# A two-layer diffusion backbone on one core: the first expert layer adds its gated results straight to the stored tokens

## The chip, the core and the metric

The kernel runs on one core of one Trainium2 chip. The metric is the device time of one execution in microseconds (us), the median of the runs; lower is better. Five engines work side by side: PE (TensorE, matmuls), DVE (VectorE), ACT (ScalarE), POOL (GpSimd) and SP (SyncE, which here only issues DMAs). SBUF is the memory on the core, PSUM holds what matmuls write, DRAM is the chip's large memory.

## The reference

768 tokens of 1024 numbers (256 context tokens, then 512 latent ones) pass through two layers. Each layer has a mixer (attention) and a mixture of 32 experts, of which every token uses two. Cut to what matters here:

```python
for l in range(2):
    x = x + gt1 * o_lat                       # mixer; ctx likewise with cgt1 where not last
    if l == 0:
        tokens = concat([modulate(ctx, ...csh2, csc2), modulate(x, ...sh2, sc2)])
        f = hier_moe(tokens, ...)             # 768 tokens
        ctx = ctx + cgt2 * f[:256]            # the context's gate row
        x = x + gt2 * f[256:]                 # the latent tokens' gate row
    else:
        f = hier_moe(modulate(x, ...), ...)   # 512 tokens
        x = x + gt2 * f
# hier_moe: y = (silu(x @ w1[e]) * (x @ w3[e])) @ w2[e];  f = sum over the token's two experts of weight * y
```

The two gate rows cgt2 and gt2 hold 1024 numbers each, one per column. A token's gate depends only on whether it is a context or a latent token, so gating each expert's result before the sum gives the same f as gating the sum.

## The kernel before

Tokens lie in SBUF as `oo`, six tiles of 128 tokens (tiles 0 and 1 are context). Stages, by the time of the profile: first mixer (0 to 400 us), its output projection with the router (to 494), MoE of layer 0 (to about 1042), a hand-over, second mixer `mixer_c` (differential attention, to about 1470), its output projection with the router (to 1543), MoE of layer 1 (to the end).

**MoE.** Each expert has 6 MB of weights (w1, w3, w2), which stream from DRAM through slots of 1 MB (`wr`, `oo` reused). An expert with up to 64 tokens is "small": its tokens are gathered as half rows (128 x 512, tiles `xg`); eight others, the two "static" ones first and six "big" ones, are gathered as 96 rows of 1024 (`xgb`). Per expert: POOL gathers the rows by an indirect DMA (`gather`, L1518); PE transposes them (`trx`), DVE or ACT copies them out (`x`); PE multiplies with w1 and w3 (`h`); ACT takes silu (`sl`), DVE the product (`gp`); PE transposes (`trg`), then multiplies with w2 (`py`, two PSUM buffers); `weigh` multiplies with the tokens' router weight, from PSUM to `y` in SBUF; POOL scatters `y` by an indirect DMA that adds (`scatter`, L1525). Scatters of one layer wait for one another's landing, since they add to the same DRAM tensor. In layer 0 `weigh` is one ACT instruction per 512 columns (L1532) and the scatter adds to `yd`, a DRAM tensor of sums that was set to zero early in the kernel (`no_sums`, L836). In layer 1 `weigh` is one DVE instruction that also multiplies with the gate row (L1534), and the scatter adds straight to the output, which holds the tokens by then.

**Hand-over.** `xd` (`source(1, t)`) is DRAM with the tokens as they were before MoE 0. Near the end of MoE 0 the ACT queue loads them back to `oo` (six DMAs of 512 KB, L1722) and SP loads the two gate rows (`next_rows`, L505) and the first weights of `mixer_c` (`next_weights`, L1743). A branch follows that joins all engines (`overflow`, L1757; its body, for experts that overflow their table, does not run here). Then `mixer_c` (L1851 to L1910) loads the sums from `yd`, multiplies them by the gates (DVE for tile 0, POOL for tiles 1 to 5, L1886), adds them to `oo` (DVE, L1889), stores the four latent tiles back to `xd` (L1904), squares and sums each tile (ACT, L1892), finds the reciprocal root (`rstd`, nine small DVE instructions, L285 to L297), scales (ACT, L1910), and `flip_mod` transposes the tile on PE (`ht`, L646), modulates it (`h`, L655/L657) and splits it in two parts of matmul operands (`chh`, `chl`). With the first column blocks of the weights split in the same way (`wh`, `wl`, L323) PE starts the projections (`pp`, L262 to L264).

**Order.** Within each stage a list scheduler in the kernel's own code (`Sched`) writes the instruction order of PE, DVE, ACT and POOL: every step has an engine, an assumed time, the steps that it depends on, a due position (`S.pos`), and buffers that it takes and gives. SP's DMAs keep the order of the code. Each engine runs its list strictly in order.

Of the kernel before, what the change touches and what calls it, by code (L numbers as in the profile page):

```python
# [12 lines left out]
I32 = mybir.dt.int32  # L13
# [35 lines left out]
GATES = 1  # L49
# [187 lines left out]
class Backbone:  # L237
# [94 lines left out]
    def setup(self):  # L332
# [26 lines left out]
        self.yd = [tc.dram_tile([NTOK, D], F32, name="yd")]  # L359
# [409 lines left out]
    def mixer_ab(self):  # L769
# [52 lines left out]
        def second_stage():  # L822
# [7 lines left out]
            c.zero = one.tile([128, 64], F32, name="zero")  # L830
            nc.sync.dma_start(c.sink, i["sink_a"][0].partition_broadcast(128))
            nc.gpsimd.tensor_scalar(c.nsink, c.sink, -1.0, None, op0=OP.mult)
            nc.gpsimd.memset(c.zero, 0.0)
# [37 lines left out]
        for t in range(NT):  # L871
            S.op("DMA", 0.1, lambda t=t: no_sums(t), [closed], pos=n - APREP + t)
# [148 lines left out]
    def prepare_out(self, l, wout, pos, after):  # L1021
# [6 lines left out]
        def room():  # L1028
# [3 lines left out]
                "idx": t("idx", [128, NST], I32), "sw": t("sw", [128, NST]), "ps": t("ps", [CAP, 2, NE]),  # L1032
                "ord": t("ord", [1, NE], I32), "idx2": t("idx2", [128, NE], I32), "sw2": t("sw2", [128, NE]),
                "idxb": t("idxb", [CAP, 8], I32), "swb": t("swb", [CAP, 8]), "base": t("base", [128, NE]), "nb": t("nb", [NE, 2]), "ad": t("ad", [128, 2 * NT], I32),
# [30 lines left out]
    def out_proj(self, l, oo, first, gain=None):  # L1065
# [10 lines left out]
        with ExitStack() as st:  # L1076
# [158 lines left out]
            def index():  # L1235
# [4 lines left out]
                V.tensor_copy(r["sw"][:CAP], pslot[:, 1, 0:NST])  # L1240
                nc.scalar.copy(r["ps"], pslot)

# [66 lines left out]
    def route(self, l, j, nt, x, v, deps, sb, psp, pslot, summed, placed):  # L1309
# [5 lines left out]
        def t(name, *sh):  # L1315
            if name not in T:
                T[name] = sb.tile([128, *sh], F32, tag="r_" + name, name=name)
            return T[name]
# [59 lines left out]


    def sort_experts(self, l, nt):  # L1380
        nc, V, cst, r = self.nc, self.nc.vector, self.cst, self.rt
        with tc_pools(self.tc, ("sos", 1, {}), ("sop", 1, {"space": PSUM})) as (sb, ps):
# [28 lines left out]
            nc.scalar.copy(r["sw2"], p2[:, 1])  # L1411
# [3 lines left out]
            nc.scalar.copy(r["swb"], p3[:, 1])  # L1415
# [74 lines left out]
    def moe(self, l, nt, oo):  # L1490
# [3 lines left out]
        with ExitStack() as st:  # L1494
# [7 lines left out]
            gate = None  # L1502
            if l == 1:
                gate = one.tile([128, DE], F32, name="g2"), one.tile([CAP, D], F32, name="g2b")
                for h in range(2):
                    nc.sync.dma_start(gate[0][CS * h:CS * h + CS],
                                      self.modrow[1][0, 5 * D + DE * h:5 * D + DE * h + DE].partition_broadcast(CS))
                nc.sync.dma_start(gate[1], self.modrow[1][0, 5 * D:6 * D].partition_broadcast(CAP))
            xgs = [one.tile([128, DE], F32, name=f"xg{j}") for j in range(NX)]
            xgb = [one.tile([CAP, D], F32, name=f"xgb{j}") for j in range(2)]  # L1510
# [602 lines left out]
```

## Time and profile before

| what | value |
|---|---|
| median of 3 runs | 2069.01 us (2067.35 to 2069.65) |
| profiled execution | 2068.61 us |
| its span in the trace | 2066.8 us |
| busy: PE / DVE / ACT / POOL | 1795.9 / 935.4 / 561.1 / 336.2 us |
| DMA moved | 541 MB, mean 262 GB/s |

The span is what the trace covers from the first to the last record; 1.8 us of the profiled execution lie outside it. All times in the rows are of the profiled execution, counted from the span's start. A row of the timeline gives start, duration, engine, line, operation, output<-inputs, the count of like instructions, and in brackets the idle time before it and what ended it. "ACTq" or "SPq" mark the queue part of an engine, which issues DMAs; there the duration is the time of issuing, not of the transfer. A row of a window gives its length, then the busy time of each engine in it (with counts), the clock that TensorE was granted (1.00 is its upper level), the busy share of the DMA engines and what they moved. MoE stages are bounded by the weight stream, mixers by PE; how far that holds for the stretches that the change touches is in the rows below.

### The profile page before, as it was taken

How to read it: one execution, taken by the hardware profiler on the slowest of the kernel's cores; microseconds unless marked ns; L12 is line 12 of the kernel's file. 1: busy time of each engine (PE TensorE's matmuls, PEld its weight loads, DVE VectorE, ACT ScalarE, POOL GpSimd, SP SyncE). 2: the span in 40 equal slices, each digit the busy share in tenths (PEclk: the TensorE clock that was granted, in tenths of full speed). 3: DMA queues.
4: the chain of work that ended last, by engine and by line, in shares of the span. 5: the costliest groups of instructions: out<-in, count | busy, mean ns of one | idle time of the engine just before them, and what ended most of it. 6: DMA issues, size and time to landing. Idle time of an engine off the chain costs nothing. (4 is left out here: it accounts for less than half of the span.)

```text
span 2066.8 us, 26429 instructions
## 1 busy us (share of the span) xinstructions
PE 1795.9 (87%) x9506; PEld 1060.8 (51%) x9506; DVE 935.4 (45%) x2496; ACT 561.1 (27%) x1281; POOL 336.2 (16%) x358
## 2 busy tenths in 40 slices
PE   4999998896999988989838999996878998898896
PEld 2798776684333332323327988886763332232232
DVE  4698878585111111111168878776781211111111
ACT  4564566321001000001045555554310000000000
POOL 2000000002112111111042322224121211111111
PEclk8999999897999999999969999998988999999999
DMA  8702314437899999999952223231449999999996
GB/s 331 261 25 91 123 45 163 154 133 260 333 381 394 407 402 404 396 408 406 369 194 75 72 85 129 74 116 36 179 182 356 357 397 413 411 412 414 413 412 262
DMA packets 111016, 541.23 MB, mean 262 GB/s; under 512 B 34451, under 2 KB 34819, under 8 KB 55585
## 3 DMA queue, kind: packets, MB, share of 16 engines
q1 hardware_dynamic: 95584, 515.30, 63.7%
q0 software_dynamic: 14432, 21.05, 4.3%
q10 hardware_dynamic: 864, 3.15, 0.4%
q8 instruction: 77, 1.26, 0.2%
q14 instruction: 59, 0.48, 0.1%
HBM read 521.12 MB, written 34.28 MB: 269 GB/s over the span
## 5 line engine op out<-in xcount | busy, mean ns | idle before, releaser
L1628 PE MATMUL h<-wr,x 128*64 128x512 f32 x1584 | 405.1, 606 | 70.1 <-DMA wr<-in_w_dram 69.8
L1628 PEld LDWEIGHTS h<-wr,x 128*64 128x64 f32 x1584 | 117.0, 137 | 284.6 <-issue 158.6
L1603 DVE COPY x<-trx 128x512 f32<-128x512 f32 (+1 forms) x74 | 47.4, 649 | 457.2 <-PE trx L1598 452.4
L1652 ACT ACTIVATE sl<-h 64x512 f32<-64x512 f32 (+1 forms) x64 | 37.8, 590 | 694.1 <-PE h L1628 485.2
L1626 PE MATMUL h<-wr,x 128*96 128x512 f32 x416 | 191.7, 613 | 10.4 <-DMA wr<-in_w_dram 10.4
L1687 PE MATMUL py<-wr,gt 128*64 128x512 f32 x816 | 190.1, 600 | 7.8 <-DMA wr<-in_w_dram 6.6
L1657 DVE TENSOR_TENSOR gp<-sl,h 64x512 f32<-64x512 f32 (+1 forms) x64 | 67.7, 1058 | 242.5 <-ACT sl L1652 159.8
L262 PE MATMUL pp<-wh,chh 128*128 128x384 f32 (+1 forms) x384 | 132.7, 345 | 4.8 <-ACT chh L323 2.5
L1626 PEld LDWEIGHTS h<-wr,x 128*96 128x96 f32 x416 | 67.9, 169 | 116.7 <-issue 110.5
L264 PE MATMUL pp<-wh,chl 128*128 128x384 f32 (+1 forms) x384 | 123.8, 322 | 1.1 <-DVE chl L326 1.1
L263 PE MATMUL pp<-wl,chh 128*128 128x384 f32 (+1 forms) x384 | 123.6, 322 | 0.0
L1687 PEld LDWEIGHTS py<-wr,gt 128*64 128x64 f32 x816 | 57.8, 138 | 127.4 <-issue 103.3
L620 PE MATMUL ptp<-cst,p 128*128 128x128 f32 x592 | 97.3, 286 | 25.7 <-DVE p L1987 12.7
L1518 POOL DMA_INDIRECT xg<-h2d,ridx x51 | 53.7, 1053 | 246.2 <-PE trx L1598 242.9
L620 PEld LDWEIGHTS ptp<-cst,p 128*128 128x128 f32 x592 | 70.4, 145 | 44.8 <-issue 18.2
L1685 PE MATMUL py<-wr,gt 128*96 128x512 f32 x208 | 92.2, 596 | 0.1
L1525 POOL DMA_INDIRECT out_dram<-y,ridx x29 | 45.6, 1571 | 239.7 <-DVE y L1534 236.3
L262 PEld LDWEIGHTS pp<-wh,chh 128*128 128x128 f32 x384 | 73.8, 192 | 15.8 <-ACT vv L689 7.1
L951 ACT ACTIVATE p<-s,nbias,r 128x256 f32<-128x256 f32 (+3 forms) x96 | 76.5, 800 | 18.3 <-DVE nbias L945 8.0
L1525 POOL DMA_INDIRECT yd<-y,ridx x26 | 40.8, 1570 | 246.2 <-ACT y L1532 239.0
L1198 POOL TENSOR_TENSOR h2p<-xi,bc 128x512 f32<-128x512 f32 x10 | 16.7, 1667 | 375.7 <-DVE xi L1195 321.7
L624 ACT COPY pts<-ptp 128x384 f32<-128x384 f32 (+2 forms) x112 | 54.0, 487 | 75.3 <-PE ptp L620 74.7
(351 smaller groups left out, 3342.2 us busy)
## 6 DMA issues: line engine op xcount, KB each, us to landing
wr<-in_w_dram SPq DMA_DIRECT2D x378, 1024.0 KB
wr<-in_w_mod_dram SPq DMA_DIRECT2D x48, 1024.0 KB
wr<-in_wc_dram SPq DMA_DIRECT2D x16, 768.0 KB
wr<-in_wab_dram SPq DMA_DIRECT2D x8, 768.0 KB
oo<-in_w_dram SPq DMA_DIRECT2D x6, 1024.0 KB
xd<-oo SPq DMA_DIRECT2D x10, 512.0 KB
h2d<-h2p SPq DMA_DIRECT2D x10, 512.0 KB
bc<-modrow SPq DMA_DIRECT2D x9, 512.0 KB
```

Source lines behind the costliest of these rows:

```text
L262: mm(ps, xh, wh, start=start, stop=False)
L263: mm(ps, xh, wl, start=False, stop=False)
L264: mm(ps, xl, wh, start=False, stop=stop)
L620: nc.tensor.transpose(st[g][:, b], st["p"][:, (g + b) * 128:(g + b + 1) * 128], self.id)
L624: f(st["pts"][:, g:g + n], st[g][:, :n])
L951: nc.scalar.activation(p[:, a:b], st["s"][:, a:b], AF.Exp, bias=nb()[:, m:m + 1], scale=hr()[:, m:m + 1], accum_out=z["ssum"][:, h + m:h + ...
L1525: nc.gpsimd.indirect_dma_start(out=dst, out_offset=bass.IndirectOffsetOnAxis(ap=idx, axis=0), in_=src, in_offset=None, bounds_check=(tok i ...
L1626: mm(x["h"][m][:CAP], x["k"](k), w, start=k == 0, stop=k == KD - 1)
L1628: mm(x["h"][0][CS * m:CS * m + CS], x["k"](k), w, start=k == 0, stop=k == KD - 1, tile_position=(0, CS * m), skip_group_check=True)
L1657: nc.vector.tensor_tensor(x["p"][:n].rearrange("t (k p) -> t p k", k=4), v(x["s"][:n]), v(x["h"][1][:n] if isb else x["h"][0][CS:128]), op ...
L1685: mm(x["y"][m][:CAP], x["gt"][:, k], w, start=k == 0, stop=k == 3)
L1687: mm(x["y"][0][CS * m:CS * m + CS], x["gt"][:, k, 0:CS], w, start=k == 0, stop=k == 3, tile_position=(0, CS * m), skip_group_check=True)
```

## The change

`yd`, its zeroing and its loads go. In MoE 0 the scatter adds to `xd` itself. `weigh` becomes three DVE instructions in layer 0: result x weight x latent gate, result x weight x context gate (to a scratch tile `yc`), and their sum. Each token's router weight is stored twice for that (`by_kind`): once as it is for latent tokens and zero for context ones, and once the other way round. Both gate rows are loaded at the start of MoE 0, six DMAs on SP ahead of the first weights, and stay there. To make room there is one `xgb` buffer instead of two, in both layers. The hand-over loses the gate rows and the ACT queue's loads of `oo`; `mixer_c` loads the finished tokens from `xd` behind the branch, squares a whole tile in one instruction, scales it in place, and has no gate, no add and no store. The rope tables (`rope_tables`, POOL) no longer wait for the gates.

```diff
-        def no_sums(t):
-            nc.sync.dma_start(self.yd[0][t * 128:(t + 1) * 128].rearrange("p (a b) -> p a b", a=16),
-                              c.zero[:, None, :].to_broadcast([128, 16, 64]))
...
+    def by_kind(self, l, sw, ids, w):
+        V = self.nc.vector
+        if l:
+            V.tensor_copy(sw[:, 0], w)
+            return
+        V.tensor_scalar(sw[:, 1], ids, float(CTX) + 0.5, None, op0=OP.is_gt)
+        V.tensor_tensor(sw[:, 0], w, sw[:, 1], op=OP.mult)
+        V.tensor_tensor(sw[:, 1], w, sw[:, 0], op=OP.subtract)
...
-            gate = None
-            if l == 1:
-                gate = one.tile([128, DE], F32, name="g2"), one.tile([CAP, D], F32, name="g2b")
+            gates = []
+            for v in range(1 if l else 2):
+                gate = one.tile([128, DE], F32, name=f"g2_{v}"), one.tile([CAP, D], F32, name=f"g2b_{v}")
                 for h in range(2):
                     nc.sync.dma_start(gate[0][CS * h:CS * h + CS],
...
-            xgb = [one.tile([CAP, D], F32, name=f"xgb{j}") for j in range(2)]
+            xgb = [one.tile([CAP, D], F32, name="xgb")]
...
-            sums = self.out[0] if l else self.yd[0]
+            sums = self.out[0] if l else self.xd
...
             def weigh(dst, src, sw, cs, big):
+                n = src.shape[0]
+                g = [a[1][:n, cs] if big else a[0] for a in gates]
+                nc.vector.scalar_tensor_tensor(dst, src, sw[:, 0], g[0], op0=OP.mult, op1=OP.mult)
                 if l == 0:
-                    nc.scalar.activation(dst, src, AF.Copy, scale=sw)
-                else:
-                    nc.vector.scalar_tensor_tensor(dst, src, sw, gate[1][:, cs] if big else gate[0], op0=OP.mult, op1=OP.mult)
+                    t = sb.tile([128, DE], F32, tag="yc", name="yc", bufs=1)[:n]
+                    nc.vector.scalar_tensor_tensor(t, src, sw[:, 1], g[1], op0=OP.mult, op1=OP.mult)
+                    nc.vector.tensor_tensor(dst, dst, t, op=OP.add)
...
-            if l == 0:
-                for t in range(NT):
-                    S.op("ACT", 0.06, lambda t=t: nc.scalar.dma_start(oo[:, t], self.source(1, t)), [W[NE - 1, "w1", 1][1]], pos=10.0 * NE - 12.0)
...
-                self.ready = self.next_rows(), self.next_weights(i["wc"], 0)
+                self.ready = self.next_weights(i["wc"], 0)
...
+        sd = [S.op("DMA", 1.5, lambda t=t: nc.sync.dma_start(oo[:, t], self.source(1, t)), [ld]) for t in range(NT)]
...
+            X, ss = oo[:, t], one.tile([128, 2], F32, name=f"css{t}")
+            sq = S.op("ACT", 1.2, lambda: nc.scalar.activation(
+                c.hh[:, :, s], X.rearrange("p (k f) -> p k f", k=KD), AF.Square, accum_out=ss[:, 0:1]), [sd[t]])
+            r = self.rstd(lambda: (ss[:, 1:2], ss[:, 0:1]), D, [sq], once=t < ONCE)
+            xs = [S.op("ACT", 0.6, lambda m=m: nc.scalar.activation(
+                X[:, 512 * m:512 * m + 512], X[:, 512 * m:512 * m + 512], AF.Copy, scale=ss[:, 1:2]), [r]) for m in range(2)]
...
-        tables = S.op("POOL", 4.0, tables, used, pos=-24.0)
+        tables = S.op("POOL", 4.0, tables, [], pos=-24.0)
```

Where the scheduler writes another order, three places matter. POOL at the start of MoE 0 before (`xgb_5678` and `xgb_5679` are the two buffers, `ridx` the index table of the static experts, `ridxb` that of the big ones):

```order
L1512 MEMSET xgb_5678 96x1024
L1512 MEMSET xgb_5679 96x1024
L1518 DMA xgb_5678<-h2d_89,ridx 96x1024
L1518 DMA xgb_5679<-h2d_89,ridx 96x1024
L1518 DMA xg_5675<-h2d_89,ridx_3700 128x512
L1518 DMA xg_5676<-h2d_89,ridx_3700 128x512
L1518 DMA xg_5677<-h2d_89,ridx_3700 128x512
L1518 DMA xgb_5678<-h2d_89,ridxb 96x1024
```

And now:

```order
L1514 MEMSET xgb 96x1024
L1520 DMA xgb<-h2d_89,ridx 96x1024
L1520 DMA xg_5682<-h2d_89,ridx_3696 128x512
L1520 DMA xg_5683<-h2d_89,ridx_3696 128x512
L1520 DMA xg_5684<-h2d_89,ridx_3696 128x512
L1520 DMA xgb<-h2d_89,ridx 96x1024
L1520 DMA xgb<-h2d_89,ridxb 96x1024
```

The second static expert's gather stood right behind the first; now it stands behind three gathers of small experts, and waits for the first static's transposes to be done with the one buffer.

PE at the same place before (`trx` are transposes of gathered rows, `h` the matmuls with w1 and w3 of the first static expert):

```order
L1598 MATMUL trx<-cst,xgb_5678 128x96 x8
L1598 MATMUL trx<-cst,xgb_5679 128x96 x4
L1626 MATMUL h<-wr,x 96x512 x8
L1598 MATMUL trx<-cst,xgb_5679 128x96 x4
L1626 MATMUL h<-wr,x 96x512 x8
```

And now:

```order
L1603 MATMUL trx<-cst,xgb 128x96 x8
L1631 MATMUL h<-wr,x 96x512 x8
L1603 MATMUL trx<-cst,xgb 128x96 x8
L1631 MATMUL h<-wr,x 96x512 x8
L1603 MATMUL trx<-cst,xg_5682 128x128 x4
```

The second static's eight transposes, of which four stood ahead of the first matmuls, all stand between the two halves of the first static's matmuls.

ACT at the hand-over before (up to the branch):

```order
L1722 DMA oo<-xd 128x1024 x2
L1532 ACTIVATE y<-py,rsw_3701 128x512
L1722 DMA oo<-xd 128x1024 x4
L1652 ACTIVATE sl<-h 64x512
L1532 ACTIVATE y<-py,rswb 96x512 x2
L323 CAST wh<-wr 128x768 x2
L1532 ACTIVATE y<-py,rsw_3701 128x512
L323 CAST wh<-wr 128x768 x2
```

And now, behind the branch (`css` are the sums of squares, `a_1_84` and `mcol_82` the modulation):

```order
L322 CAST wh<-wr 128x768 x4
L1851 ACTIVATE chh,css_8204<-oo 128x8x128
L1851 ACTIVATE chh,css_8205<-oo 128x8x128
L1851 ACTIVATE chh,css_8206<-oo 128x8x128
L1854 ACTIVATE oo<-oo,css_8204 128x512 x2
L1854 ACTIVATE oo<-oo,css_8205 128x512
L653 ACTIVATE h<-ht,mcol_82,a_1_84 128x128 x2
```

The DMA issues and the two weightings by `y<-py` have left ACT; the casts of `mixer_c`'s first weights stood ahead of the branch and now stand behind it, and the squares of three tiles stand ahead of the first scaling.

## Rows read from the trace of the kernel before

**Rows 1.** Windows: length, busy PE, PEld, DVE, ACT, POOL; PEclk, DMA share, GB/s

```profile
640.00:1000.00 360.00, 319.75 (x1240) 111.88 (x1237) 48.92 (x69) 31.29 (x49) 52.03 (x39) 0.99 1.02 403
1046.00:1100.00 54.00, 21.98 (x121) 19.59 (x121) 44.51 (x126) 28.76 (x66) 24.11 (x28) 0.69 0.47 170
1110.00:1400.00 290.00, 281.81 (x1929) 254.40 (x1928) 228.22 (x649) 153.32 (x380) 73.63 (x115) 1.00 0.29 99
```

**Rows 2.** A window at the start, then TensorE's waits from 44 to 130 us

```profile
45.00:65.00 20.00, 18.83 (x112) 16.36 (x110) 13.01 (x28) 14.06 (x32) 0.28 (x1) 0.87 0.99 247
...
PE pmod L383 <- issue: 1.2, 1, 1.2
```

**Rows 3.** Single lines: the weighting of both MoE layers, ns min/median/max

```profile
L1532 ACT ACTIVATE y<-py,rsw x28: 682/687/689, 548.7 to 1038.4; 128x512 f32<-128x512 f32 x24, 96x512 f32<-96x512 f32 x4
...
L1534 DVE SCALAR_TENSOR_TENSOR y<-py,rsw,g x27: 750/751/752, 1625.0 to 2057.4; 128x512 f32<-128x512 f32 x27
```

**Rows 4.** Timeline: second gather and first matmuls, MoE 0, then MoE 1

```profile
496.37 0.98 POOL L1518 DMA_INDIRECT xgb<-h2d,ridx  x1 [0.30 <-issue]
...
506.25 1.51 PE L1598 MATMUL trx<-cst,xgb 96*128 96x96 f32 x8 [4.96 <-DMA wr<-in_w_dram]
509.06 0.90 PE L1598 MATMUL trx<-cst,xgb 96*128 96x96 f32 x4 [1.29 <-DMA xgb<-h2d,ridx]
509.75 9.27 PE L1626 MATMUL h<-wr,x 128*96 128x512 f32 x16
...
1546.87 1.06 POOL L1518 DMA_INDIRECT xgb<-h2d,ridx  x1 [0.17 <-POOL xgb L1512]
...
1555.61 1.51 PE L1598 MATMUL trx<-cst,xgb 96*128 96x96 f32 x8 [4.71 <-DMA xgb<-h2d,ridx]
```

**Rows 5.** Timeline of SP at the start of MoE 1, then a window of MoE 0

```profile
1544.49 0.57 SPq L1508 DMA_DIRECT2D g2b<-modrow  x1
...
530.00:570.00 40.00, 40.00 (x130) 14.82 (x130) 4.45 (x6) 3.91 (x6) 4.54 (x4) 1.00 0.86 316
```

**Rows 6.** Timelines of ACT, PE, POOL and SP, end of MoE 0 to mixer C

```profile
1022.75 7.25 ACTq L1722 DMA_DIRECT2D oo<-xd  x4
1030.11 0.59 ACT L1652 ACTIVATE sl<-h 64x512 f32<-64x512 f32 x1 [17.92 <-DMA wr<-in_wc_dram]
...
1020.35 7.08 PE L1685 MATMUL py<-wr,gt 128*96 128x512 f32 x16
1033.08 5.33 PE L1687 MATMUL py<-wr,gt 128*64 128x512 f32 x16 [0.56 <-issue]
...
1032.12 1.42 POOL L1525 DMA_INDIRECT yd<-y,ridxb  x1 [18.10 <-ACT y L1532]
1040.70 1.57 POOL L1525 DMA_INDIRECT yd<-y,ridx  x1 [7.16 <-ACTq L1757]
...
1046.14 0.81 SPq L1851 DMA_DIRECT2D wr<-yd  x2
```

**Rows 7.** Start of mixer C: VectorE and TensorE by time

```profile
1050.18 1.29 DVE L1886 TENSOR_TENSOR wr<-wr 128x512 f32<-128x512 f32 x2 [8.47 <-DMA wr<-yd]
...
1064.70 1.97 PE L646 MATMUL ht<-cst,wr 128*128 128x128 f32 x8 [26.29 <-ACT wr L1910]
...
1098.25 1.97 PE L646 MATMUL ht<-cst,y 128*128 128x128 f32 x8 [3.14 <-ACT y L1910]
```

**Rows 8.** VectorE's additions (busy us, mean ns), one rstd line, one table instruction of POOL

```profile
L1889 DVE TENSOR_TENSOR oo<-oo,y 128x512 f32<-128x512 f32 x8 | 5.9, 745 | 0.0
L1889 DVE TENSOR_TENSOR oo<-oo,wr 128x512 f32<-128x512 f32 x4 | 5.9, 1508 | 0.0
...
L297 DVE SCALAR_TENSOR_TENSOR css<-rsq,rsy x6: 149/154/1186, 1062.7 to 1096.9; 128x1 f32<-128x1 f32 x6
...
1068.46 0.46 POOL L543 TENSOR_TENSOR rs_q<-cst,nw_q 128x128 f32<-128x128 f32 x1
```

**Rows 9.** The square of a whole tile in the first mixer, ns min/median/max

```profile
L804 ACT ACTIVATE hl<-oo x6: 1039/1040/1057, 8.9 to 17.4; 128x1024 fp32r<-128x1024 f32 x6
```

More of the change, by code (lines that the diff above doesn't have):

```diff
@@ L48 @@
 NP = 3
-GATES = 1
 ONCE = 1
@@ L1316, in t @@
             if name not in T:
[L1317 removed]
+                T[name] = sb.tile([128, *sh], F32, tag="r_" + name, name=name, bufs=1 if name in ("prod", "pk") else 2)
             return T[name]
@@ L1703, in out @@
                             weigh(x["o"], x["y"][0], x["sw"], cs, False)
-                    outs.append(S.op("DVE" if l else "ACT", 0.62, out, [last["second"]] + outs,
+                    outs.append(S.op("DVE", 0.8 if l else 2.2, out, [last["second"]] + outs,
                                      take=() if m else ("yb",) if isb else ("y",), give=("py",)))
@@ L1873, in mixer_c @@
         c.tab = lambda g: c.tabs
-        hdone, used, spare = {}, [], []
+        hdone, spare = {}, []
         def tokens(t):
-            v, s = 0 if t >= NCT else 1, slice(t * 128, (t + 1) * 128)
-            X, ss = oo[:, t], one.tile([128, 4], F32, name=f"css{t}")
-            sq, xs, adds = [], [], []
-            for m in range(2):
-                cs = slice(512 * m, 512 * m + 512)
-                def gate(e, m=m, cs=cs):
-                    (nc.gpsimd if e == "POOL" else nc.vector).tensor_tensor(ys[t][m], ys[t][m], g2[0][:, v, cs], op=OP.mult)
-                def add(m=m, cs=cs):
-                    nc.vector.tensor_tensor(X[:, cs], X[:, cs], ys[t][m], op=OP.add)
-                def square(m=m, cs=cs):
-                    nc.scalar.activation(c.hh[:, 4 * m:4 * m + 4, s], X[:, cs].rearrange("p (k f) -> p k f", k=4), AF.Square,
-                                         accum_out=ss[:, m:m + 1])
-                e = "DVE" if t < GATES else "POOL"
-                a = S.op(e, 0.62 if t < GATES else 1.32, lambda e=e, gate=gate: gate(e), [gd, sd[t]])
-                used.append(a)
-                adds.append(S.op("DVE", 0.62, add, [a]))
-                sq.append(S.op("ACT", 0.7, square, [adds[m]]))
-            def keep():
-                self.dump(f"x1_{t}", X)
-                if t >= NCT:
-                    nc.sync.dma_start(self.source(1, t), X)
-            kept = S.op("DMA", 1.5, keep, adds)
-            a = S.op("DVE", 0.08, lambda: nc.vector.tensor_tensor(ss[:, 2:3], ss[:, 0:1], ss[:, 1:2], op=OP.add), sq)
-            r = self.rstd(lambda: (ss[:, 3:4], ss[:, 2:3]), D, [a], once=t < ONCE)
-            for m in range(2):
-                xs.append(S.op("ACT", 0.6, lambda m=m: nc.scalar.activation(
-                    ys[t][m], X[:, 512 * m:512 * m + 512], AF.Copy, scale=ss[:, 3:4]), [r]))
```

73 lines of the change are left out of this document (21 added, 52 removed).

## The prediction

> **What bounds the kernel now.** I read the windows first, stage by stage. In the body of MoE 0 the DMA engines are busy throughout (share 1.02, 403 GB/s) while PE works 319.75 of 360 us: the weight stream is the limit there, and DVE (48.92 us) and ACT (31.29 us) are mostly free. In the hand-over, from 1046 to 1100, PE works 21.98 of 54 us and DVE 44.51: PE starves for 32 us while DVE prepares the tokens. From 1110 to 1400 PE works 281.81 of 290 us, so whatever PE gains or loses before 1110 goes through to the end [rows 1]. The chain of waits that ended last is of no use here (it covers only the kernel's last moments), so I followed the hand-over in the timelines: the last scatter is issued at 1040.70, its sum is loaded back from 1046.14 [rows 6], the first load is used at 1050.18, the first transposition of a tile runs at 1064.70, the last at 1098.25 [rows 7]. So there are three places to price: the start of each MoE, the end of MoE 0, and the ramp of the second mixer. The ramp is by far the largest.
>
> **The zeroing (removed).** Six DMAs write zeros between 44 and 64 us; there the DMA engines are 0.99 busy at only 247 GB/s, against 403 at share 1.02 in MoE 0 [rows 1, 2]. But PE works 18.83 of these 20 us, and its longest wait from 44 to 130 us is 1.2 us of issue, not a DMA [rows 2]. A transfer that nobody waits for is worth little: I take -0.5 us, between -1.5 and 0.
>
> **The weighting in MoE 0 (ACT to DVE).** Before, 0.687 us on ACT per 512 columns; a gated weighting on DVE takes 0.751 in layer 1 [rows 3], and an addition of 128 x 512 takes 0.745 [rows 8]. Three instructions are then 2 x 0.75 + 0.745 = 2.2 us, 1.5 us later than before, for each of 24 small experts, and 4.5 us for each of the eight others, whose result has two halves: 24 x 2.2 + 8 x 4.5 = 89 us more on DVE. What hides it: DVE is busy 14% of the body of MoE 0 (48.92 of 360), and the stream of weights, not PE, sets the pace there [rows 1]. There are two `py` buffers; one expert's 16 matmuls take 5.33 to 7.08 us [rows 6], so the buffer that is freed 1.5 us later is not asked for yet. I take 0. If that cover were gone, it would be up to 1.5 us per small expert and more per big one: the slower rival below.
>
> **The start of both MoEs.** In layer 0, six gate DMAs stand ahead of the weights on SP's queue. One of them takes 0.57 us to issue in layer 1 [rows 5], so about 3.5 us, and 1.28 MB at 403 GB/s is 3.2 us of transfer. Later in MoE 0 the DMA engines have idle time while PE works without a gap (from 530 to 570 PE 40.00 of 40 us, share 0.86) [rows 5]: at the share of 1.02 seen later these 40 us have some 6 us to spare, so the delayed stream catches up before it becomes the limit. The single gather buffer costs more. The second static's gather can go only when the first's transposes are done, and its own transposes now stand between the two halves of the first's matmuls (the order above). A gather takes 8.7 us (1546.87 to 1555.61) to 12.7 us (496.37 to 509.06) from its issue to the transposes. What lies beside it is 9.27 us of matmuls [rows 4] and about 1 us of copying ahead of them. Set against each other that is -1.6 (no wait) to 12.7 + 1 (transposes to issue) - 10.3 = 3.4 us, and 1 us more for eight transposes there in place of four. Against that, the first matmuls no longer wait for the second gather: before, they began 3.5 us after the first transposes (506.25, 509.75); with 1.5 us of transposes and a copy, that can be 1 us sooner [rows 4]. I take +0.5 in layer 0, between -1.5 and +4.5, and 0 in layer 1, between -1.5 and +2.5, where the shorter flight was seen.
>
> **The end of MoE 0.** The ACT queue's loads of `oo` keep ACT from 1022.75 to 1030.00, and the last expert's silu runs only at 1030.11. PE finished the big expert's `py` at 1027.43 and could start the last one only at 1033.08 [rows 6]. Without the loads silu runs about 8 us earlier, so the last `py` can follow the big one at once, at about 1027.5: 5.5 us sooner. But the last scatter has to wait until the big expert's scatter, issued at 1032.12, has landed. That one was held to 1031.8 by ACT as well. Now its six DVE instructions end at 1027.43 + 4.5 = 1031.9: the same time. So most of the 5.5 us is lost again, and what is left is a shorter landing, since 4 MB (six tiles and two gate rows) less are in flight. Before, 8.6 us lay between the two scatters (1032.12, 1040.70); a gather's 8.7 us is the short flight seen, a landing of 5.4 us (1040.70 to 1046.14) is what the last one took with little beside it [rows 6]. I take -1.5 us, between -3.5 and +1.
>
> **The ramp of the second mixer.** Call t0 the end of the join (1046.14). Before, the first tile: loaded at +4.0, transposed at +18.6; the last transposed at +52.1 [rows 6, 7]. Of DVE's 44.51 us, 11.8 are the twelve additions, four of them at 1.51 us each where POOL multiplied gates at the same time, and small instructions of `rstd` took up to 1.19 us where the median is 0.15 [rows 1, 8]. After: two small loads stand ahead on SP (0.8 us), the first tile lands at +4.8, the next ones 512 KB / 403 GB/s = 1.3 us apart [rows 1]. ACT squares three tiles before it scales the first (the order above), each 1.04 us [rows 9], as the tiles land: at 4.8, 6.1 and 7.4, so the third ends at 8.5. `rstd` of the first tile runs beside the second and third square. Two scalings of 128 x 512 at ACT's 0.69 us [rows 3] end at +9.9: the first transposition comes 18.6 - 9.9 = 8.7 us sooner. After that the pace counts. Before, it was 33.55 us for five tiles, 6.7 each. DVE's remaining work is at most 44.51 - 11.8 = 32.7 us for six tiles, 5.4 each; ACT's is about the old 28.76 us, 4.8 each [rows 1]. Five tiles at 4.8 to 5.4 are 24 to 27 us, so the last transposition comes at +34 to +37 in place of +52.1: 15 to 18 us sooner. There is a ceiling: PE waits some 14 us at least until the first projection (9.9, then an estimated 4 for transposing, modulating and splitting by the durations of such steps), and of 32 us of idle time that leaves 18 to be won. The floor is the first tile's 8.7 us with the old pace. The casts of the weights, now behind the branch, run in the 4.8 us in which the first tile is under way; should they not fit, they cost a few tenths. I take -15 us, between -18 and -8.7.
>
> A rule speaks against this step. Additions on DVE of 0.745 us took 1.51 beside POOL's multiplications, and an `rstd` instruction up to 1.19 in place of 0.15 [rows 8]; POOL's rope tables, which waited for the gates before, can now run at once, beside the first `rstd`. The Trainium skill (SBUF — State Buffer, "Who interferes with whom") says that a DVE instruction with two inputs in SBUF and a GpSimd instruction that reads SBUF share a read port, and that the one that starts first keeps the other out until it ends; the trace agrees with its slowed additions. A table instruction takes 0.46 us [rows 8]. If six of the nine `rstd` instructions each waited for one, a `rstd` of 9 x 0.15 = 1.4 us would become 4.2, of which the second and third square, up to +8.5, cover 2.7: the ramp would lose up to 1.5 us and the sum be -15.0; with no such waits it stays as below. I take it at 0 and leave the 1.5 us to the range.
>
> **The sum.** -0.5 + 0 + 0.5 + 0 - 1.5 - 15 = -16.5 us. The profiled execution took 2068.6 us, of which 2066.8 are span; nothing outside the span changes. 2068.6 - 16.5 = 2052.1. The median, 2069.0, is 0.4 above the profiled execution, inside the spread of the runs, so I predict 2052 for the median too.
>
> **The rivals.**
> - *The old pace stays.* Only the first tile comes sooner: DVE's and ACT's steps for one tile take turns (transposition, modulation, split), and that chain, not their busy time, sets 6.7 us a tile. For it: DVE was busy 44.51 and ACT 28.76 of the 54 us, so part of the pace was waiting for each other. Against it: the additions and slowed steps stood in DVE's list between the tiles. -8.7 - 1.5 = about -10: 2059.
> - *The one gather buffer stalls PE at both starts.* +4.5 and +2.5 in place of +0.5 and 0, all else as forecast: -16.5 + 6.5 = -10: 2059. For it: the 12.7 us flight in layer 0. Against it: the first matmuls start sooner, and in layer 1 the flight was 8.7.
> - *The ramp is not shortened.* The change does what it says but the tokens, loaded only behind the join in one queue, arrive as late as the sums did, and the splits and rope tables set PE's start. Then only the end of MoE 0 and the zeroing are left: 2067, within 0.2%. Against it: the first sum was there at +4.0 and was not what PE waited for 14 us later.
> - *Slower: the three-step weighting holds `py`.* If PE has to wait for a `py` buffer at each expert, or DVE's copies for PE queue behind a weighting, the price is 1.5 us x 24 + 3.1 x 8 = 61 us in the extreme; half of it already outweighs the gain: -16.5 + 30 = about 2082, and in full 2113. It decides from 0.5 us per expert (16.5 / 32). For it: DVE's list is strict, and what PE needs can stand behind 4.5 us of a big expert's weighting. Against it: PE has 40 us of slack in the 360 us of rows 1, and DVE will be at 14% + 89/540 = about 30%.
>
> **How the numbers follow.** The forecast 0.70 (own range 2047 to 2057), the old pace 0.11, the gather 0.08, no shorter ramp 0.05, slower 0.06. About 0.2%, 4 us, is what a measurement of this kernel can tell from no change. Faster: 0.70 + 0.11 + 0.08 = 0.89; same 0.05; slower 0.06. The terms' bounds together are wider than they will ever be at once (-26 to about -0.7 us); to hold 8 of 10 I take 2044 (most of the best ends) to 2061, which takes in the two cases at 2059.
>
> **What would show it.** Right: the first `ht` transposition about 10 us after the first load of `oo` in the second mixer, the last at about +36; PE's idle time from the join to its continuous work about 16 us where it was 32; MoE 0 of the same length within 3 us, with DVE at about 30% and PE's waits still for weights; no PE wait over 3.5 us for `xgb`. Wrong: PE waits for `y` or `py` in MoE 0, a first transposition later than +14, or MoE 1 longer than before by more than 2.5 us.

## The result and the profile after

The changed kernel takes 2057.26 us (median of 5 runs, 2055.03 to 2060.83) against 2069.01 before (2067.35 to 2070.73): a ratio of 0.9945, 95% interval 0.9931 to 0.9960, or 11.75 us less. The forecast was 2052 (2044 to 2061), 16.5 us less in the profiled execution. Sign and range hold; the single terms do not. One execution below, the profiled one of `e2_big_earlier`, took 2985 us at a mean granted clock of 0.556, and no row is taken from it.

The spans of the two profiled executions differ by 11.3 us (2066.8 and 2055.5). Cut at the same instructions in both (counted from 0: the 360th score matmul `s`, the 475th `py` matmul; then the first DMA behind the join, the first score matmul of the second mixer, the last `pop` matmul of its output projection, the first and last `py` of MoE 1), they divide like this:

| stretch | before | after | difference | forecast |
|---|---|---|---|---|
| start to the 360th `s` (first mixer) | 369.69 | 366.70 | -3.0 | -0.5 |
| to the 475th `py` (MoE 0) | 640.32 | 643.14 | +2.8 | +0.5 |
| to the join (tail of MoE 0) | 36.13 | 31.65 | -4.5 | -1.5 |
| to the first `s` of the second mixer (ramp) | 80.62 | 75.38 | -5.2 | -15 |
| to the last `pop` | 400.35 | 399.76 | -0.6 | 0 |
| to the first `py` of MoE 1 | 64.06 | 60.67 | -3.4 | 0 |
| to the end | 475.62 | 478.14 | +2.5 | 0 |

The first two rows are not to be taken at their face: in the runs below, which share the first mixer, the 240th `s` fell anywhere between 263.1 and 266.6 us (265.99 before), and the second row between 640.2 and 643.9 where MoE 0 is the changed kernel's. The tail (31.1 to 31.8 us), the ramp (73.8 to 75.4) and MoE 1's start (60.7 to 62.4) come out nearly the same in the runs that leave them as they are.

**The ramp.** Two windows, columns as in [rows 1], first of the kernel before, then of the changed one, each from the join to the first score matmul:

```profile
1046.14:1126.76 80.62, 47.25 (x280) 41.67 (x281) 66.11 (x186) 41.03 (x94) 35.25 (x46) 0.78 0.46 160
```

```profile
1041.49:1116.87 75.38, 49.07 (x280) 43.58 (x281) 51.35 (x166) 42.77 (x86) 18.18 (x36) 0.79 0.33 119
```

DVE lost 14.8 us of work and POOL 17.1. PE's idle time fell by 7.1 us, from 33.4 to 26.3, but its 280 instructions take 1.8 us longer, which leaves the 5.2. Timelines of SP, ACT and PE there:

```profile
1041.49 0.34 SPq L528 DMA_DIRECT2D nw_q<-in_qn_c_dram  x1
1041.88 0.42 SPq L528 DMA_DIRECT2D nw_k<-in_kn_c_dram  x1
1042.41 3.34 SPq L1837 DMA_DIRECT2D oo<-xd  x6
...
1048.66 1.06 ACT L1851 ACTIVATE chh<-oo 128x1024 fp32r<-128x1024 f32 x1 [3.97 <-DMA oo<-xd]
...
1052.78 1.97 PE L644 MATMUL ht<-cst,oo 128*128 128x128 f32 x8 [22.45 <-ACT oo L1854]
...
1080.13 0.66 PE L644 MATMUL ht<-cst,oo 128*128 128x128 f32 x4 [2.88 <-ACT h L653]
1082.61 1.12 PE L644 MATMUL ht<-cst,oo 128*128 128x128 f32 x4 [1.82 <-ACT oo L1854]
```

The first transposition comes 11.3 us after the join (18.6 before, [rows 7]), that of the last tile 38.6 after it (52.1), and that of the last tile's second half 41.1 (53.0). So the first tile gained 7.3 us and the last 13.5. But PE's gain is 5.2. Its longest waits in that window, total, times, longest (the one of 22.4 us began before the join):

```profile
PE ht L644 <- ACT oo L1854: 29.6, 4, 22.4
PE ht L644 <- ACT h L653: 2.9, 1, 2.9
PE pp L261 <- POOL sub L1868: 1.9, 1, 1.9
```

Counted in the single records, PE was idle 11.3 us up to the first transposition and 12.9 between it and the last; before, 18.6 and 13.2. The whole gain is the first tile's; between the tiles nothing was won, though they come faster. In that stretch PE's list now holds less work. Here are the projections (`pp`) alone, from the join to the first transposition of the last tile (length, busy PE, PEld, ACT), first before, then in the changed kernel:

```profile
1046.14:1098.25 52.11, 13.83 (x72) 12.36 (x72) 0.84 (x4) 0.70 0.49 176
```

```profile
1041.49:1080.13 38.64, 9.17 (x48) 8.32 (x48) 0.41 (x2) 0.67 0.35 135
```

Of the 198 projections up to the first score, 72 stood ahead of the last tile and 48 do now; the other 24 have moved behind it. The longer matmuls go with the clock. The granted clock fell to its lower level, 0.5, at 1080.7 us, behind PE's wait of 2.9 us, and the 24 projections behind the last half tile took 6.3 us; in `e1_tokens_first` below the same 24 took 4.5 us at 1.00. The two windows:

```profile
1083.38:1089.70 6.32, 6.32 (x26) 5.99 (x24) 5.75 (x20) 2.05 (x5) 2.71 (x6) 0.68 0.01 5
```

```profile
1079.89:1084.35 4.46, 4.46 (x27) 4.13 (x25) 3.92 (x9) 2.35 (x5) 2.56 (x6) 1.00 0.00 0
```

**The tail of MoE 0.** PE, then POOL of the changed kernel; the lines of before are [rows 6]:

```profile
1018.72 7.11 PE L1690 MATMUL py<-wr,gt 128*96 128x512 f32 x16
1026.68 3.65 PE L1692 MATMUL py<-wr,gt 128*64 128x512 f32 x16 [0.46 <-ACT gt L1672]
...
1029.45 1.42 POOL L1527 DMA_INDIRECT xd<-y,ridxb  x1 [14.15 <-DVE y L1539]
1035.58 1.56 POOL L1527 DMA_INDIRECT xd<-y,ridx  x1 [4.70 <-DMA xd<-y,ridxb]
```

As forecast, the last `py` follows the big one at once. The big expert's scatter goes out 3.6 us behind the end of its `py` (4.7 before), and the last scatter follows it after 6.1 us (8.6 before): the forecast's -1.5 was too little.

**The start of MoE 1.** POOL, then PE of the changed kernel:

```profile
1525.71 1.48 POOL L1514 MEMSET xg<- 128x512 f32 x3 [1.08 <-DVE gm L1322]
1533.98 1.07 POOL L1520 DMA_INDIRECT xgb<-h2d,ridx  x1 [5.90 <-DVE rsw L1372]
1544.39 0.98 POOL L1520 DMA_INDIRECT xgb<-h2d,ridx  x1 [2.86 <-PE trx L1603]
...
1542.61 1.51 PE L1603 MATMUL trx<-cst,xgb 96*128 96x96 f32 x8 [2.88 <-DMA wr<-in_w_dram]
1544.19 9.12 PE L1631 MATMUL h<-wr,x 128*96 128x512 f32 x16
1553.15 0.83 PE L1603 MATMUL trx<-cst,xgb 96*128 96x96 f32 x8
```

Beside those of [rows 4], two lines of before, POOL and PE:

```profile
1543.43 1.45 POOL L1512 MEMSET xg<- 128x512 f32 x3 [8.34 <-DVE rsw L1240]
...
1559.20 8.50 PE L1626 MATMUL h<-wr,x 128*96 128x512 f32 x16
```

The matmuls start 1.6 us after the first transpositions (3.6 before, here in MoE 1). The first transpositions, too, come 2.5 us sooner behind the last `pop` (26.0 us for 28.5): POOL clears the buffers (MEMSET) while it waits for the router's tables, where before it began to clear only behind `rsw`, so that the first gather went 3.4 us later than the clearing began. Up to the first `py` 1.1 of these 4.5 us are lost again. The second gather has 8.8 us until its transpositions, and the 9.12 us of matmuls cover it: no wait stands at the last line. In MoE 0 PE waited 0.8 us for it:

```profile
513.28 0.88 PE L1603 MATMUL trx<-cst,xgb 96*128 96x96 f32 x8 [0.78 <-DMA xgb<-h2d,ridx]
```

### The profile page after: what moved, and what is told of

It is laid out like the page before. It is cut to its first block, busy times and chain, and to the rows that moved or that the text cites. A ratio compares the mean times of both kernels' runs of the same rounds, so it can differ in the third digit from the quotient of the medians.

```text
span 2055.5 us, 26431 instructions
## 1 busy us (share of the span) xinstructions
PE 1803.5 (88%) x9506; PEld 1063.1 (52%) x9506; DVE 984.2 (48%) x2572; ACT 547.7 (27%) x1259; POOL 316.7 (15%) x345
## 5 line engine op out<-in xcount | busy, mean ns | idle before, releaser
L1633 PE MATMUL h<-wr,x 128*64 128x512 f32 x1584 | 402.9, 612 | 62.5 <-DMA wr<-in_w_dram 62.4
L1631 PE MATMUL h<-wr,x 128*96 128x512 f32 x416 | 203.7, 645 | 18.7 <-DMA wr<-in_w_dram 18.4
L1657 ACT ACTIVATE sl<-h 64x512 f32<-64x512 f32 (+1 forms) x64 | 37.9, 592 | 666.3 <-PE h L1633 468.0
L1672 ACT COPY gt<-trg 128x256 f32<-128x256 f32 (+1 forms) x55 | 21.7, 394 | 239.4 <-PE trg L1668 239.4
L1535 DVE SCALAR_TENSOR_TENSOR y<-py,rsw,g 128x512 f32<-128x512 f32 x51 | 38.3, 751 | 97.1 <-PE py L1692 95.4
```

The costliest lines, as they stand in the source:

```text
L1631: mm(x["h"][m][:CAP], x["k"](k), w, start=k == 0, stop=k == KD - 1)
L1633: mm(x["h"][0][CS * m:CS * m + CS], x["k"](k), w, start=k == 0, stop=k == KD - 1, tile_position=(0, CS * m), skip_group_check=True)
```

## The experiments

Each run gives a median beside the kernel before on the same chip (2069.0 to 2070.0 there). "The changed kernel" is 2057.26; as the runs are spread over several chips, a difference from it is good to about 1 us besides its spread.

**The token loads first** (`e1_tokens_first`).

```diff
-        tables = S.op("POOL", 4.0, tables, [], pos=-24.0)
+        tables = S.op("POOL", 4.0, tables, sd, pos=-24.0)
```

> In the changed kernel the two loads of rope norm weights stand ahead of the token loads behind the join, and the DMA engines move only 11 to 112 GB/s from 1042 to 1045 us; the first square starts 7.2 us after the join, against the first use of a sum 4.0 us after it before. Here the token loads go first. Theory (the two small broadcast loads hold the queue): the first square comes 4.0 to 5.0 us after the join, the first transposition at +8.5 to +9.5 in place of +11.3, and the kernel is 2 to 3 us faster than the changed one. Rival (the delay is the first read behind the scatter or the DMA start itself): the first square stays at about +7 and the time does not change. Second rival: the rope tables on POOL now run beside more of VectorE's work and slow it, so that less than 1 us is left of the gain.

2053.72 us, ratio to before 0.9928 (0.9910 to 0.9946): 3.5 us faster than the changed kernel. First a window of the changed kernel, then the same window of this run, then its timeline of SP and ACT:

```profile
1043.00:1044.00 1.00, 0.00 (x0) 0.00 (x0) 1.00 (x2) 1.00 (x3) 0.00 (x0) 0.50 0.36 48
```

```profile
1043.00:1044.00 1.00, 0.00 (x0) 0.00 (x0) 0.93 (x2) 1.00 (x3) 0.00 (x0) 0.50 0.96 365
```

```profile
1041.45 2.75 SPq L1837 DMA_DIRECT2D oo<-xd  x6
1045.10 0.33 SPq L528 DMA_DIRECT2D nw_q<-in_qn_c_dram  x1
...
1045.61 1.06 ACT L1851 ACTIVATE chh<-oo 128x1024 fp32r<-128x1024 f32 x1 [0.36 <-issue]
```

With the same join (1041.45) the first square starts at +4.2 in place of +7.2, the first transposition at +9.1, and the ramp takes 71.1 us. The two loads of 32 KB, which the forecast priced at 0.8 us of issuing, cost 3 us, because little moves while they run (48 against 365 GB/s). Of the ramp's 4.3 us, 2.2 are the first tile's and 0.9 shorter matmuls at the upper clock; the other 1.2 are idle time behind the first tile. The rope tables beside more of DVE's work took nothing of it back.

**One engine for a half tile's modulation** (`e8_one_engine_h`), in the second mixer:

```diff
-            js = [S.op(("DVE", "ACT"), (0.2, 0.25), lambda e, j=j, affine=affine: affine(e, j), [a]) for j in range(4)]
+                js = [S.op(("DVE", "ACT"), (0.8, 1.0), lambda e, affine=affine: [affine(e, j) for j in range(4)], [a])]
```

> In the second mixer the modulation of a transposed half tile (four pieces) is shared by VectorE and ScalarE, and each waits about 0.5 us for the other at every change (0.59 and 0.48 us idle). Here one engine does all four of a half tile. Theory (this taking of turns, not the engines' busy time, sets the pace of 6 us a tile): the tiles come 0.5 to 1 us closer together and the kernel is 2 to 5 us faster. Rival (ScalarE's squares and scalings set the pace): the spacing of the transpositions changes by less than 0.3 us and the time by under 1 us.

2050.59 us, ratio 0.9913 (0.9896 to 0.9929): 6.7 us faster than the changed kernel. A part of the second tile in the changed kernel, DVE and ACT, then in this run:

```profile
1061.43 0.41 DVE L655 TENSOR_SCALAR h<-ht,a,mcol 128x128 f32<-128x128 f32 x1 [0.59 <-ACT h L653]
1062.81 0.73 DVE L655 TENSOR_SCALAR h<-ht,a,mcol 128x128 f32<-128x128 f32 x2 [0.59 <-ACT h L653]
...
1061.88 0.90 ACT L653 ACTIVATE h<-ht,mcol,a 128x128 f32<-128x128 f32 x2 [0.48 <-DVE h L655]
```

```profile
1061.69 1.37 DVE L655 TENSOR_SCALAR h<-ht,a,mcol 128x128 f32<-128x128 f32 x4 [0.80 <-PE ht L644]
...
1062.55 1.51 ACT L653 ACTIVATE h<-ht,mcol,a 128x128 f32<-128x128 f32 x4 [2.10 <-PE ht L644]
```

In the changed kernel the 48 pieces of the ramp (four to a half tile) go to the two engines by turns, and at 16 changes one waits for the other (total, times, longest, from the join to 1090 us):

```profile
DVE h L655 <- ACT h L653: 4.7, 8, 0.6
ACT h L653 <- DVE h L655: 5.5, 8, 1.7
```

In this run no piece waits for the other engine: four pieces are one stretch, and two halves run side by side. The ramp falls from 75.4 to 68.2 us. PE's idle time in it falls from 26.3 to 21.6; the other 2.5 us are shorter matmuls, as the granted clock stays at 1.00 from 1074.8 us on. The even spacing that I expected is not there: the last tile's first transposition comes 37.9 us after the join (38.6 in the changed kernel), its second half's 38.3 (41.1). And the edit changed PE's list as well. Its projections ahead of the last tile, 48 in the changed kernel, are 66:

```profile
1041.90:1079.78 37.88, 13.37 (x66) 12.30 (x66) 0.84 (x4) 0.66 0.37 145
```

So what is shown is that the turns, together with the order that the scheduler writes around them, held 6.7 us. How much of it is the waits' and how much PE's order no run tells apart.

**The same edit in the kernel before** (`e9_before_h`).

> The kernel before with the one edit of one engine for the modulation of a half tile in the second mixer. Theory (taking turns set the pace in both kernels, so that the removed additions could not speed it up): 3 to 7 us faster than before. Rival (before, VectorE's additions and the gates set the pace, and turns did not matter): under 1.5 us.

2066.36 us, ratio 0.9985 (0.9975 to 0.9995): 3.2 us faster, at the lower end of the theory's range, with an interval of 1.0 to 5.2. The ramp takes 79.2 us (80.6), so only 1.5 us of the gain lie there, which is the rival's edge. The turns themselves were as many before: 14 waits of 9.1 us in all, against 16 and 10.2. A reading that fits is that before, most of their cost lay behind DVE's additions and slowed steps, and that the change, which took those away, raised it from 1.5 to 7.2 us of the ramp. That is argued, not shown: these are single profiled executions, and PE's order differs here too.

**A busy TensorE in the hand-over** (`e7_warm`): the first loop behind the last expert of MoE 0, the second at the start of the second mixer:

```diff
+            for _ in range(10):
+                mm(p, self.id, self.cst[:, 0:512], start=True, stop=True)
...
+            for _ in range(8):
+                nc.tensor.matmul(p, self.id, self.cst[:, 0:512], start=True, stop=True)
```

> Adds matmuls whose result nobody reads: 10 behind the last expert of MoE 0 (some 9 us, in the wait for the join) and 8 at the start of the second mixer (7 us at the upper clock, before the first tile comes). Theory (part of the ramp's missing gain is TensorE's clock, which was 0.5 from 1033 to 1064 us): the granted clock is 1.0 at the first projections, TensorE's busy time from the join to the first scores falls from 50.4 to under 48 us, and the kernel is 1 to 4 us faster. Rival (TensorE waits for the tiles anyway, the clock only moves idle time): the clock is up but the time changes by less than 0.5 us.

2058.09 us, ratio 0.9947 (0.9930 to 0.9964): no gain; the ramp takes 75.2 us. Two windows of this run:

```profile
1043.88:1050.00 6.12, 4.86 (x12) 1.88 (x10) 3.57 (x4) 3.03 (x4) 1.94 (x4) 1.00 0.56 187
1050.00:1064.00 14.00, 6.29 (x26) 5.63 (x27) 8.41 (x39) 9.46 (x17) 3.88 (x10) 0.58 0.75 291
```

The clock was at its upper level during the added matmuls, but back to 0.58 in the mean once PE waited for the first tile. PE's own work in the ramp is no shorter (49.4 us in the single records, 49.2 in the changed kernel). So this does not show what the ramp would take at the full clock; it shows that these 18 matmuls do not buy it.

**Big experts one position earlier** (`e2_big_earlier`).

```diff
-                if j % every == every // 2 and big:
+                if j % every == every // 2 - (l == 0) and big:
```

> The last two experts of MoE 0 in the changed kernel are a big one and a small one; the small one's result is ready at 1032.5 us but its scatter waits until 1035.6 for the big one's to land. Here each big expert of layer 0 comes one position earlier, so that two small ones stand at the end. Theory (the order of the landings holds the join): the last scatter goes out within 0.5 us of its result, and the join comes about 3 us earlier. Rival (the last scatter is held by the small expert before it in the same way): the join moves by less than 1 us. Between the two: the small expert's scatter is 5 to 6 us in flight too, but starts some 7 us earlier than the big one's.

2055.1 us in its four other executions (2055.39 with the long one), ratio 0.9933 (0.9916 to 0.9950), some 2 us faster than the changed kernel, which these intervals hardly tell from nothing. The last run below has the same edit and shows the place.

**The loads on the ACT queue put back** (`e11_act_loads`).

```diff
+            if l == 0:
+                for t in range(NT):
+                    S.op("ACT", 0.06, lambda t=t: nc.scalar.dma_start(oo[:, t], self.h2d[0][128 * t:128 * t + 128]), [W[NE - 1, "w1", 1][1]], pos=10.0 * NE - 12.0)
```

> The changed kernel with six loads of 512 KB put back on the ACT queue near the end of MoE 0 (from another DRAM tensor; what they load is overwritten behind the join). In ACT's list they stand ahead of the last big expert's copy and the last silu. Theory (these loads, by holding ACT and by their traffic, made the old tail): from the 475th second-weight matmul to the join it takes 36 us or more in place of 31.7, and the kernel is 4 to 6 us slower than the changed one. Rival (the tail is shorter for the other reasons, the gate rows and the place of the weighting): under 1.5 us.

2064.70 us, ratio 0.9978 (0.9969 to 0.9988): 7.4 us slower than the changed kernel. ACT and PE:

```profile
1007.28 17.68 ACTq L1726 DMA_DIRECT2D oo<-h2d  x6
1025.05 0.48 ACT L1672 COPY gt<-trg 128x384 f32<-128x384 f32 x1 [17.40 <-DMA wr<-in_w_dram]
...
1025.58 9.33 PE L1690 MATMUL py<-wr,gt 128*96 128x512 f32 x16 [5.35 <-ACT gt L1672]
```

The tail takes 40.5 us in place of 31.7 (36.1 before). It overshoots the kernel before, since here a copy that PE waits for stands behind the loads. That loads on ACT's queue hold ACT and with it the tail is shown; how much of the old tail came from holding ACT and how much from the traffic is not.

**The gates twice, and half of them** (`e5_gates_twice`: each gate load of layer 0 issued twice; `e10_one_gate`: only the latent rows).

```diff
+                for rep in range(1 if l else 2):
```

```diff
-            for v in range(1 if l else 2):
+            for v in range(1):
...
+            if l == 0:
+                gates.append(gates[0])
```

> The changed kernel with each of the gate loads of layer 0 issued twice: 1.28 MB and six DMAs more ahead of the weights of MoE 0. Theory (the gates' bytes are paid in full, because the weight stream limits MoE 0 and has no slack to give): the last experts of MoE 0 come 3 us later and the kernel is 3 us slower. Rival (the prediction's: the stream catches up between 530 and 570 us): under 1 us.

> The changed kernel with only the latent gate rows loaded in layer 0 and used for both kinds of token, 0.64 MB and three DMAs fewer; context tokens get the wrong gate. The second copy of all gates cost 4 to 5 us. If the first copy costs as much per byte, MoE 0's last experts come 1.5 to 2.5 us earlier than in the changed kernel (the 475th second-weight matmul at 1007.5 to 1008.5 us); if the first copy is covered by idle time of the DMA engines between 530 and 570 us, it stays at 1009.8 to 1011.

Twice: 2062.19 us, ratio 0.9964 (0.9950 to 0.9978), 4.9 us slower; the 475th `py` comes at 1015.27. Half: 2059.71, ratio 0.9951 (0.9934 to 0.9967); the 475th `py` at 1012.09, against 1009.84 in the changed kernel and 1010.0 to 1012.1 in the other runs with its MoE 0: not sooner, nor is the kernel faster. The spread of that instruction is as wide as the 1.5 to 2.5 us looked for, so this test is a weak one. From 530 to 570 us, in the changed kernel, with the gates twice, and with half of them:

```profile
530.00:570.00 40.00, 40.00 (x138) 14.67 (x138) 10.29 (x14) 3.64 (x7) 5.04 (x4) 1.00 0.91 350
```

```profile
530.00:570.00 40.00, 40.00 (x132) 14.79 (x132) 10.29 (x14) 3.20 (x6) 3.56 (x3) 1.00 1.02 413
```

```profile
530.00:570.00 40.00, 40.00 (x132) 14.79 (x132) 10.28 (x14) 3.20 (x6) 3.60 (x4) 1.00 0.80 295
```

The idle share of the DMA engines there takes up the first copy (0.86 before, [rows 5]); with two it is used up, and the rest is paid. This is the cover that the forecast named, with its end in sight. My expectation that the bytes are always paid held for the second copy and fell for the first. That the price is the bytes' alone is not shown: 1.28 MB at 403 GB/s are 3.2 us, not 4.9, and with two copies SP waits, by the profile, 5.4 us in all for first copies to land, among its first weight loads.

**The single gather buffer alone** (`e4_before_one_xgb`), in the kernel before:

```diff
-            xgb = [one.tile([CAP, D], F32, name=f"xgb{j}") for j in range(2)]
+            xgb = [one.tile([CAP, D], F32, name="xgb")]
```

> The kernel before with the one edit of a single gather buffer for 96 rows. Theory (the single buffer makes the starts of both MoEs faster, because the first matmuls no longer wait for the second gather): MoE 1 starts its second-weight matmuls 3 to 3.5 us earlier relative to its router, of which 1 to 2 us are left at the end, since the weight stream takes over; MoE 0 gains 1 to 2 at its start. In all 1 to 3 us faster than before. Rival (the prediction's: the single buffer stalls TensorE): 0.5 to 7 us slower.

2070.0 us, ratio 1.0003 (0.9994 to 1.0013): nothing at the end. But from the last `pop` to the first `py` of MoE 1 it takes 60.8 us, as in the changed kernel (64.1 before), and from there to the last `py` 468.1 (465.6 before). The earlier start is the buffer's doing, and the rest of MoE 1 takes 2.5 of 3.3 us back, 1.8 of them in PE's waits for weights (48.2 us for 46.4).

**The zeroing put back** (`e3_zeroing`: the six DMAs and their zero tile in the changed kernel).

```diff
+            S.op("DMA", 0.1, lambda t=t: no_sums(t), [closed], pos=n - APREP + t)
```

> The changed kernel with the zeroing of a DRAM tensor put back at its old place (nothing adds to it). Theory (the zeroing cost the first mixer its 1.9 to 3 us, though no wait there named it): the k-th score matmul of the first mixer comes 1.9 us later from 85 us on and 2.9 us later from 240 us on than in the changed kernel, as in the kernel before; what reaches the end is 1 to 2 us. Rival (that shift is from another order or chance): under 0.5 us.

2058.48 us, ratio 0.9947 (0.9930 to 0.9963), 1.2 us slower, inside the spread of the runs. The 240th `s` came at 264.1; in runs without the zeroing it came between 263.1 and 266.6. So the 3 us that the first mixer seems to gain in the table are not the zeroing's: they come and go between executions of one and the same code.

**One weighting instruction** (`e6_one_weigh`).

```diff
-                if l == 0:
-                    t = sb.tile([128, DE], F32, tag="yc", name="yc", bufs=1)[:n]
-                    nc.vector.scalar_tensor_tensor(t, src, sw[:, 1], g[1], op0=OP.mult, op1=OP.mult)
-                    nc.vector.tensor_tensor(dst, dst, t, op=OP.add)
```

> The changed kernel with one weighting instruction per 512 columns in MoE 0 in place of three: it leaves out the context's gate, so that context tokens get nothing from the experts of layer 0. Theory (the three instructions cost nothing in the body and only the tail's scatter): body of MoE 0 the same within 0.5 us; the big expert's scatter goes out 3 us earlier and the join comes 1.5 to 3 us earlier. Rival (VectorE's 89 us more hold the body): the last experts come more than 1 us earlier too.

2058.31 us, ratio 0.9947 (0.9931 to 0.9964): no gain. MoE 0's body is as long (640.9 us to the 475th `py`, within the other runs' 640.2 to 643.9). The big scatter goes out 2.6 us sooner (17.1 us after the 475th `py`, not 19.6), yet the last one comes at the same 25.8: it waited 8.8 us for the big one's landing in place of 6.1. DVE has 51 us less to do in MoE 0 (97.0 us up to the join, 147.6 in the changed kernel), and nothing comes of it beyond the 3.7 us by which that stretch varies: these 51 of the 66 us that the change added there (81.8 before) are free. And a big scatter that goes out sooner does not by itself shorten the tail.

**Three edits together** (`c2_tokens_h_big`: those of `e1_tokens_first`, `e8_one_engine_h` and `e2_big_earlier`).

```diff
+        tables = S.op("POOL", 4.0, tables, sd, pos=-24.0)
...
+                js = [S.op(("DVE", "ACT"), (0.8, 1.0), lambda e, affine=affine: [affine(e, j) for j in range(4)], [a])]
...
+                if j % every == every // 2 - (l == 0) and big:
```

> The changed kernel with three edits together: token loads ahead of the rope norm weights (3.5 us by medians alone), one engine for the modulation of a half tile (6.7 us), big experts of layer 0 one position earlier (1.9 us). If the three gains are on different parts of one chain they add up: 2057.3 - 12.1 = 2045, between 2043 and 2048. If the first two buy the same idle time of TensorE, the sum is 2 to 3 us short: about 2048.

2044.27 us, ratio 0.9881 (0.9864 to 0.9897): 25.3 us faster than before and 13.0 than the changed kernel; the gains add up. The ramp takes 66.1 us. POOL and DVE at the tail:

```profile
1023.38 1.56 POOL L1530 DMA_INDIRECT xd<-y,ridx  x1 [9.36 <-issue]
1031.62 1.56 POOL L1530 DMA_INDIRECT xd<-y,ridx  x1 [6.68 <-DMA xd<-y,ridx]
...
1027.78 0.69 DVE L1542 TENSOR_TENSOR y<-y,yc 128x512 f32<-128x512 f32 x1
```

With two small experts at the end, the last result is ready at 1028.5 and still waits 3.1 us for the scatter before it. From the 475th `py` to the join it takes 30.2 us in place of 31.7: less than the theory's 3 us and more than the rival's 1, since the landing of a small expert's scatter stays in the way. From the 360th `s` to the join it takes 668.8 us, and 671.6 to 675.5 in the runs with the other order, so the order may gain something ahead of the tail too; one profiled execution does not show it.

## Why the prediction was right, and where it was not

The time fell in the range of 2044 to 2061, at the upper edge of the forecast's own 2047 to 2057. Term by term:

- *The ramp, -15 forecast, -5.2 measured* (-5.2 to -6.8 over the runs that leave it as it is). This is the term that failed. Its first steps nearly held. The first tile gained 7.3 us for 8.7; the missing 1.4 is the small loads ahead of it, +3 for +0.8, partly made good by shorter steps behind. "Five tiles at 4.8 to 5.4 us" missed by little: from the first transposition of the first tile to that of the last it took 27.35 us, 5.5 a tile (6.7 before), so the last tile came at +38.6 for +34 to +37.
- *PE does not profit from the last tile.* This is the step that failed: I counted the last transposition's 15 to 18 us as PE's. The last tile did come 13.5 us sooner. But PE has 47 to 49 us of work from the join to the first scores, 24 of its projections moved from between the tiles to behind the last one, its idle time between the tiles stayed at 13 us, and its matmuls took 1.8 us longer. Of the idle time of 32 us I took all but 14 for winnable, without asking what PE's list would hold there; 13.5 at the last tile became 5.2. That PE's order is what kept the idle time is read from the trace of both kernels; no run changes the order alone.
- *The rival "the old pace stays"*, at 0.11, gave 2059, which is nearer to 2057.3 than 2052 is. Its condition did not hold (5.5 us a tile, not 6.7), its price did, as only the first tile's gain counted. The turns that it named do cost: e8 takes them away, with another order of PE, and gains 6.7 us.
- *The tail, -1.5 forecast, -4.5 measured*, beyond the bound of -3.5. The step "the same time" for the big scatter failed: it came 2.7 us sooner, as the big expert's `py` ended 1.6 us sooner (1025.83 for 1027.43) and the first half of its result is weighted while the last matmuls run. The next scatter could follow 2.5 us sooner behind it. e11 shows that loads on the ACT queue lengthen the tail; what the shorter landing is owed to stays open, for in e6 a big scatter 2.6 us sooner landed no sooner.
- *The single buffer, +0.5 and 0 forecast.* PE waited 0.8 us for the second gather in MoE 0 and not at all in MoE 1. It starts sooner, as "the first matmuls no longer wait" said and as POOL clears the buffers earlier, which the forecast did not see; nothing of it is left at the end (e4).
- *The gates' loads: covered*, as forecast, as far as e5 and e10 can tell.
- *The zeroing: nothing measurable* (forecast -0.5; e3). *The weighting: 0*, as forecast (e6), with 66 us more on DVE in MoE 0 where 89 were forecast; of the slower rival's waits nothing is to be seen.
- *The tables beside the first `rstd`*: the trace has one instruction of 0.35 us in place of 0.16; the 1.5 us allowed for were not needed. The small loads helped in that: they held up the first `rstd`, and the tables ended at 1051.0 us, when it was half done.

The terms' errors go both ways, 10 us too much in the ramp, 3 too little in the tail and 1 in MoE 1; that is why the total stayed in the range. It is luck in part: with the ramp as measured and all else as forecast the sum is 2068.6 - 6.7 = 2061.9, outside it.

## What to carry to other kernels

Busy time divided by items is a lower bound of a pace, not the pace: where two engines take turns on one tile, count the changes. What a late stage gains counts only so far as the waiting engine's idle time falls; count that, not the last event, and look at what the engine's list holds in the stretch that gets shorter. Behind a join, what is needed first goes first on the queue, however small the loads ahead of it are.

## What the runs showed of the hardware

Two broadcast loads of 32 KB (256 B to each of 128 partitions) ahead of the token loads kept the DMA engines at 11, 48 and 112 GB/s in three successive us, where token loads in their place moved 78, 365 and 406 (e1). A scatter that adds was 6.0 to 10.3 us in flight as the next one saw it, and its length did not follow when it was issued (e6, e4). At a change between DVE and ACT on one PSUM tile the next engine mostly waited 0.48 to 0.59 us here (16 waits of 0.2 to 1.7 us in the changed kernel's ramp); whether the chip or only the program's own dependencies ask for it was not tried.
